# Where the tiles of a two-layer diffusion backbone begin in SBUF

## The chip, the cores and the metric

The kernel runs on one core of a Trainium2 chip. The metric is the device time of one execution in microseconds (us). A profile of one execution gives every instruction's start and length on each engine: PE (matmuls), PEld (the loads of a matmul's stationary operand, which overlap with PE), DVE, ACT, POOL, and SP, which issues most DMAs in the order in which they stand in its queue.

## The reference

A trunk of two layers (`DEPTH = 2`) works on 1024 latent tokens of width 1024, with 256 context tokens ahead of them in layer 0. All is float32. Cut to what matters here:

```python
# every layer: x = x + gate * norm(mixer(modulate(norm(x)))), then the same around a ConvFFN
# layer 0 (even): two mixers side by side
def attend(q, k, v):                                   # 8 query heads, 2 key heads, 64 wide, axial rotary
    s = jnp.einsum("bqhgd,bkhd->bhgqk", q, k).astype(jnp.float32) * ATTN_SCALE
    p = jax.nn.softmax(s, axis=-1).astype(v.dtype)
    return jnp.einsum("bhgqk,bkhd->bqhgd", p, v)
def step(S, inp):                                      # HGRN2, 4 heads, both directions, chunks
    ...
    o = jnp.einsum("bhts,bhsv->bhtv", scores, vc) + jnp.einsum("bhtd,bhdv->bhtv", qc * jnp.exp(b), S)
    S_new = jnp.exp(b_last[:, :, 0, :])[..., None] * S + jnp.einsum("bhsd,bhsv->bhdv", kc * jnp.exp(b_last - b), vc)
# layer 1 (odd): neighbourhood attention, 16 heads, 8 x 16 neighbours on a 64-wide grid, learned bias
# ConvFFN: up to 2 x 2816, a depthwise convolution of width 3 over the tokens, gate squared times value, down to 1024
```

## The kernel before, in words

Float32 operands are split into a high and a low part (names end in h and l, or _hi and _lo), and each product is three matmuls: high × high, high × low and low × high, accumulated in PSUM. In the rows of the profile a matmul reads `out<-moving,stationary`. Each matmul has its own load of 128 × 128 weights. Nearly all matmuls go through the helper on line 113, so all of them have the line L113, and one has to go by the names of their tiles.

The stages follow one another in this way. Times are those of the stretches of the profiled execution:

| stretch, us | stage | matmuls that carry it |
|---|---|---|
| 0–123 | modulation from `c_in`, first norm | `mod_ps<-m_raw,csil` |
| 123–254 | token-major projections of layer 0 (queries, keys, values, inputs), `mmB` | `g_ps<-w_hi,xh` and its two companions |
| 254–734 | bidirectional recurrence (`hgrn`) with its projections, `mmA` | `g_ps<-xh,w_hi` between many small ones |
| 734–1113 | even attention; its output projection runs between heads, its tail alone at the end | `a_pt`, `a_pv`, `g_ps<-w_hi,a_oh` |
| 1160–1730 | FFN-up of layer 0 | `u_g`, `u_v`, `u_pc` |
| 1730–2010 | FFN-down of layer 0 | `d_ps<-d_Bh,d_Ah` |
| 2030–2155 | values of layer 1, `mmB` | `g_ps<-w_hi,xh` |
| 2155–2543 | neighbourhood attention with its projections, `mmA` | `c_s`, `c_pt`, `c_pv`, `g_ps<-xh,w_hi` |
| 2606–2704 | output projection of layer 1 (`out_proj`) | `g_ps<-w_hi,a_oh` |
| 2750–3205 | FFN-up of layer 1 | `u_g`, `u_v` |
| 3205–3440 | FFN-down of layer 1 | `d_ps<-d_Bh,d_Ah` |

FFN-up is a Strassen-like scheme of seven products for each of 22 values of j: A11·B11, A12·B21, S2·T2, S1·T1, S3·T3, A22·T4 and S4·B22. A are halves of the weights and S sums of them; B are quarters of the normed input and T sums of them. One product is 4 slices of 128 rows, three matmuls of 512 columns each:

```python
                self.mm(ps, h, xhk, start and i == 0, False)
                self.mm(ps, h, xlk, False, False)
                self.mm(ps, lo, xhk, False, stop and i == len(jobs) - 1)
```

So 84 matmuls of 128x512 make one j. In layer 0 the context tokens add 48 of 128x256 (`u_pc`). While PE works on one j, ACT and POOL split and add the weights of the next, and DVE adds products, applies the convolution, and squares (`f_u`, `f_t`).

The order of the instructions on PE, ACT, DVE and POOL is the order in which the program writes them (`in_order`), and each engine works through its own row. SP's queue is first in, first out. A tile's place in SBUF is set by its pool: pools are stacked, some from the left edge of SBUF and some (`side="right"`: the weights, `nx`) from the right edge, and within a pool one tile follows the other. So a small tile shifts the start of everything that is stacked behind it. The pool `const` at the far left holds `mhalf` (the exponent −0.5 of line 121); behind it, on its side, stand `small`, the modulation's tiles and each stage's.

The tiles that the change touches: `mhalf` (L70); `c_in` (L164, the conditioning vectors, loaded first of all and passed through Silu into `csil`, the stationary operand of the modulation's matmuls); `onw` (L523, the norm's weight in `hgrn`, one value per partition, read on L822 by `h_o`); `zeros` (L1019, in even attention); `cw` (L1306, the convolution's weights in FFN-up).

Of the kernel before, what the change touches and what calls it, by code (L numbers as in the profile page):

```python
# [11 lines left out]
F32 = mybir.dt.float32  # L12
# [3 lines left out]
OP = mybir.AluOpType  # L16
# [4 lines left out]
P = 128  # L21
D = 1024
KT = D // P
# [13 lines left out]
EPS = 1e-6  # L37
HGRN_SCALE = 128 ** -0.5
NEG = -1.0e30


BLOCKS = ((0, 512), (512, 512), (1024, 256))
# [2 lines left out]
def vap(t, off, dims):  # L45

    b = t[:]
    return bass.AP(tensor=b.tensor, offset=b.offset + off, ap=[list(b.ap[0])] + [list(d) for d in dims])


class Homes:

    def __init__(self, first, second, names):
        self.first, self.second, self.names = first, second, names
# [6 lines left out]
class Trunk:  # L61
    def __init__(self, tc, a, out, es):
        self.tc, self.nc, self.a, self.out = tc, tc.nc, a, out
        nc = self.nc
        pool = lambda n, b, **k: es.enter_context(tc.tile_pool(name=n, bufs=b, **k))
        self.cp = pool("const", 1)
        self.dp = pool("scratch", 1, space=DRAM)
        self.ident = self.cp.tile([P, P], F32, name="ident")
        make_identity(nc, self.ident)
        self.mhalf = self.cp.tile([P, 16], F32, name="mhalf")  # L70
        nc.vector.memset(self.mhalf, -0.5)
        self.small = pool("small", 8)
        d = lambda n, s, t=F32: self.dp.tile(s, t, name=n)
        self.q2d = d("q2d", [AQ, P, NTOK], F32R)
        self.k2d = d("k2d", [AKV, 2, P, NTOK], F32R)
        self.v2d = d("v2d", [NT, P, AKV * P], F32R)
        self.bid = d("bid", [NT, P, 512])
        self.hgd = d("hgd", [BH, P, NTOK])
        self.gated = d("gated", [DEPTH, 2, 2, D])
        self.x1d = d("x1d", [NTOK, D])  # L80
        self.x2d = d("x2d", [NTOK, D])
        self.x3d = d("x3d", [SEQ, D])
        self.actd = d("actd", [FK, P, NTOK])
        self.vcd = d("vcd", [NT, P, CH * P], F32R)
        self.ocd = d("ocd", [KT, P, SEQ])
        self.ed = d("ed", [CH, 8, 31, 24])
        self.mod = {}
        self.fill_offset = 600
        E = mybir.EngineType
        self.compute = (E.PE, E.Activation, E.DVE, E.Pool)  # L90
# [70 lines left out]
    def mod_init(self):  # L161
        nc, a = self.nc, self.a
        self.csil = self.mc.tile([P, KT, 32], F32, name="csil")
        c = self.mc.tile([P, KT, 2], F32, name="c_in")  # L164
        nc.sync.dma_start(c, a["cc"])
        nc.vector.memset(self.csil, 0.0)
        nc.scalar.activation(self.csil[:, :, 0:2], c, AF.Silu)
        self.bmt = self.mc.tile([P, DEPTH, 48], F32, name="bmt")
        nc.sync.dma_start(self.bmt, a["bmodT"])
        self.nrm = self.mc.tile([P, DEPTH, 2, KT], F32, name="nrm")  # L170
        nc.sync.dma_start(self.nrm, a["npreT"])
# [341 lines left out]
    def hgrn(self, xh, xl, gp, tp, pp, sp, mods):  # L513
# [4 lines left out]
        nc, a = self.nc, self.a  # L518
# [1 line left out]
        M2 = sp.tile([P, 5, 32], F32, name="hM2", bufs=1)  # L520
        nc.sync.dma_start(M1, a["hM1"])
        nc.sync.dma_start(M2, a["hM2"])
        onw = sp.tile([P, 1], F32, name="onw", bufs=1)  # L523
        nc.sync.dma_start(onw, a["out_norm"])
        ones = sp.tile([P, P], F32, name="ones", bufs=1)
        nc.vector.memset(ones, 1.0)
        WD = 512
# [68 lines left out]
        def chain(u):  # L596

            st = U[u]
            n, nch, F, K, q = st["n"], st["nch"], st["F"], st["K"], st["q"]
# [11 lines left out]
            while m <= 64:  # L611
                if m <= 16:
                    KM = sp.tile([P, WD], F32, name="hKM", tag="hKM", bufs=2)
                    nc.scalar.copy(vap(KM, 0, ((2 * m, n // (2 * m)), (m, 2), (1, m))),
                                   vap(K, 0, ((2 * m, n // (2 * m)), (WD + m, 2), (1, m))))
                yield
                if m == 1:
                    for c in range(nch):
                        for i in range(4):
                            b = c * P + 32 * i  # L620
                            self.mm(pd[c // 2][32 * i:32 * i + 32, c % 2, 4, :], kd[:, b:b + 32], q[:, b:b + 32], True, True,
                                    tile_position=(0, 32 * i))
                if m <= 16:
                    slot = {8: 0, 4: 1, 2: 2, 1: 3}.get(m)
                    for c in range(nch):
                        for i in range(4):
                            b = c * P + 32 * i
                            o = pa[32 * i:32 * i + 32, c, 32 * i:32 * i + 32] if m == 16 else \
                                pd[c // 2][32 * i:32 * i + 32, c % 2, slot, :]
                            self.mm(o, KM[:, b:b + 32], vap(Q, b, ((2 * m, 16 // m), (WD + m, 2), (1, m))), True, True,  # L630
                                    tile_position=(0, 32 * i))
                else:
                    for c in range(nch):
                        for b in range(0, P, 2 * m):
                            l, r = slice(b, b + m), slice(b + m, b + 2 * m)
                            gl, gr = slice(c * P + b, c * P + b + m), slice(c * P + b + m, c * P + b + 2 * m)
                            self.mm(pa[l, c, r], K[:, 0, gl], Q[:, 1, gr], True, True, tile_position=(0, b))
                            self.mm(pa[r, c, l], K[:, 1, gr], Q[:, 0, gl], True, True, tile_position=(0, b + m))

                nb = n // (2 * m)  # L640
                tt, o = (F, 0) if m == 1 else (T, toff[m])

                ko = vap(K, 0, ((WD + m, 2), (2 * m, nb), (1, m)))
                nc.vector.tensor_tensor(out=ko, in0=ko, in1=vap(tt, o + 1, ((WD - 1, 2), (2, nb), (0, m))), op=OP.mult)
                qo = vap(Q, 0, ((WD + m, 2), (2 * m, nb), (1, m)))
                nc.vector.tensor_tensor(out=qo, in0=qo, in1=vap(tt, WD + o + 1, ((-WD - 1, 2), (2, nb), (0, m))), op=OP.mult)
                nc.vector.tensor_tensor(out=vap(T, toff[2 * m], ((WD, 2), (1, nb))), in0=vap(tt, o, ((WD, 2), (2, nb))),
                                        in1=vap(tt, o + 1, ((WD, 2), (2, nb))), op=OP.mult)
                m *= 2
            tot = st["tot"] = sp.tile([P, 2, 4], F32, name="htot", bufs=3)  # L650
            nc.vector.tensor_copy(tot[:, :, :nch], vap(T, 504, ((WD, 2), (1, nch))))
            while tails:
# [21 lines left out]
            for i in range(len(pd)):  # L674
                k = min(2, nch - 2 * i)
                nc.vector.tensor_tensor(out=T5[:, 2 * i:2 * i + k], in0=pd[i][:, :k],
                                        in1=M2.unsqueeze(1).to_broadcast([P, k, 5, 32]), op=OP.mult)
# [101 lines left out]
    def hgrn_out(self, st, dirs, part, tp, pp, sp, onw, ones):  # L779
        nc = self.nc  # L780
        n0, n, nch = st["n0"], st["n"], st["nch"]
# [14 lines left out]
        if part == "keep":  # L796
            o = st["part"] = sp.tile([P, 512], F32, name="h_part", bufs=1)
# [3 lines left out]
        if part is None:  # L801
            o = sp.tile([P, 512], F32, name="h_o", bufs=1)
            nc.scalar.copy(o[:, :n], pof[:, :n])
        else:
            o = part
# [13 lines left out]
        pb = tp.tile([P, 512], F32, name="h_bc", tag="tp")  # L819
        self.mm(pb[:, :n], ones, dg.rearrange("p c n -> p (c n)")[:, :n], True, True)  # L820
        yield
        nc.vector.scalar_tensor_tensor(out=o[:, :n], in0=pb[:, :n], scalar=onw, in1=o[:, :n], op0=OP.mult, op1=OP.mult)  # L822
        nc.gpsimd.tensor_tensor(out=o[:, :n], in0=o[:, :n], in1=st["gate"][:, :n], op=OP.mult)
        yield
        nc.gpsimd.dma_start(self.hgd[st["h"]][:, n0:n0 + n], o[:, :n])
# [2 lines left out]
    def even_attention(self, gp, tp, pp, sp):  # L828
# [5 lines left out]
        nc, a = self.nc, self.a  # L834
# [181 lines left out]
                    next(fill, None)  # L1016
                    at[0] += 1

        zeros = sp.tile([P, 1], F32, name="zeros", bufs=1)  # L1019
        nc.gpsimd.memset(zeros, 0.0)  # L1020
        N = 2 * len(pairs)
        E = mybir.EngineType
# [175 lines left out]
    def ffn_up(self, l, src, ctx, x_src, x_dst, hp, pp, tp, es, beside):  # L1198


        nc, a = self.nc, self.a
# [84 lines left out]
        with self.in_order(*self.compute), ExitStack() as loads:  # L1286
# [16 lines left out]
            for f in early:  # L1303
                f()
            sp = self.pool(es, f"fu{l}", 2)
            cw = sp.tile([P, 44, 4], F32, name="cw", bufs=1)  # L1306
            nc.sync.dma_start(cw, a["convT"][l])
            load(1, 0)
            first(0)
# [7 lines left out]
            for j in range(FK):  # L1317
                n = j + 1
# [801 lines left out]
    def pool(self, es, n, b=1, **k):  # L2120
        k.setdefault("reuse_waits", "tile")
        return es.enter_context(self.tc.tile_pool(name=n, bufs=b, **k))
# [117 lines left out]
def shape_constants():  # L2240
# [21 lines left out]
    full = np.broadcast_to(rowok[:, :, None], (P, 16, 24))  # L2262
    c["rmask"] = order(np.where(full, 0.0, -NEG).astype(np.float32))
    full = np.broadcast_to(colok[:, None, :], (P, 16, 24))
    c["cmask"] = order(np.where(full, 0.0, -NEG).astype(np.float32))
    return c
# [52 lines left out]
```

## Time and profile before

| | |
|---|---|
| median of 3 runs | 3436.86 us (3434.71 to 3441.72) |
| profiled execution, span | 3440.7 us, 48748 instructions (its own time is not given beside it) |
| mean granted TensorE clock | 0.957 |
| PE busy | 91% of the span |
| weight loads busy | 75% |
| DVE, POOL, ACT busy | 60%, 44%, 43% |
| mean DMA rate | 116 GB/s |

The page gives for each engine the time in which it was busy. Matmuls overlap in the pipeline: one of 512 columns is recorded with some 0.39 us, while the next one starts after some 0.23. So what a stream of matmuls costs is read from the distance between starts, and not from the recorded length. The chain of work that ended last merges a stream of matmuls into one piece with its length and count, and length divided by count is that distance.

### The profile page before, as it was taken

To read this page: it belongs to the slowest core of one execution; us is meant where nothing else is said; L and a number is where in the kernel's file an instruction comes from. 1 tells how busy PE (TensorE), PEld (TensorE's weight loads), DVE (VectorE), ACT (ScalarE), POOL (GpSimd) and SP (SyncE) were. 2 spreads that over 40 slices of the span, in tenths; PEclk is the share of its full clock that TensorE was granted. 3 is DMA by queue.
4 is the path that set the end of the run, shared out by engine and by line. 5 is a ranking of instruction groups with operands and counts; after the bars stand their busy time and mean duration, and the time that the engine had idled before them with its cause. 6 is when DMAs were issued, how large, how long until landed. Compare 5 with 4: busy or idle time off the path is not lost.

```text
span 3440.7 us, 48748 instructions
## 1 busy us (share of the span) xinstructions
PE 3141.5 (91%) x18364; PEld 2565.3 (75%) x18364; DVE 2058.2 (60%) x3413; ACT 1486.8 (43%) x2619; POOL 1525.8 (44%) x1147
## 2 busy tenths in 40 slices
PE   5899998869998699999999989999997679999997
PEld 2767676658887488888878768898986468888785
DVE  3624666657775754544577862476775565554778
ACT  3322222256664543434344442566664343333443
POOL 1310111187774466666610111677771167777201
PEclk7999999979999799999999999999998799999998
DMA  6524333221112211212285772222216412222756
GB/s 232 154 97 136 118 127 117 101 89 38 50 44 71 96 68 62 70 68 72 74 290 193 259 233 108 70 61 64 64 45 185 138 61 80 74 86 80 266 184 217
DMA packets 203948, 399.25 MB, mean 116 GB/s; under 512 B 23216, under 2 KB 85168, under 8 KB 203712
## 3 DMA queue, kind: packets, MB, share of 16 engines
q1 hardware_dynamic: 194656, 364.15, 32.4%
q0 software_dynamic: 9056, 31.99, 2.4%
q8 instruction: 144, 2.36, 0.3%
q14 instruction: 92, 0.75, 0.1%
HBM read 322.11 MB, written 74.34 MB: 115 GB/s over the span
## 4 chain that ended last, share of the span: by engine, by line
PE 75%; DVE 10%; DMA 4%; ACT 4%; issue 4%; POOL 2%; SPq 0%; POOLq 0%; ACTq 0%; DVEq 0%
PE g_ps L113 21%; PE u_g L113 13%; PE d_ps L113 11%; PE u_v L113 10%; PE u_pc L113 3%; PE a_pv L113 2%; PE c_pv L113 2%; PE c_s L113 2%; PE c_pt L2028 2%; PE a_pt L926 2%; PE mod_ps L113 1%; DVE a_pl L928 1%; PE a_s L113 1%; ACT a_ph L927 1%; DMA y_x<-x2d 1%
## 5 line engine op out<-in xcount | busy, mean ns | idle before, releaser
L121 POOL TENSOR_TENSOR rs_r<-rs_e,mhalf 128x1 f32<-128x1 f32 (+3 forms) x106 | 81.4, 768 | 1018.4 <-DVE rs_e L120 1018.2
L113 PE MATMUL d_ps<-d_Bh,d_Ah 128*128 128x512 f32 x704 | 276.9, 393 | 11.4 <-ACT d_Bh L1456 10.9
L113 PE MATMUL g_ps<-xh,w_hi 128*128 128x512 f32 (+1 forms) x704 | 278.8, 396 | 4.4 <-ACT w_hi L543 4.4
L113 PE MATMUL d_ps<-d_Bl,d_Ah 128*128 128x512 f32 x704 | 277.6, 394 | 2.9 <-DVE d_Bl L1457 2.4
L113 PE MATMUL d_ps<-d_Bh,d_Al 128*128 128x512 f32 x704 | 276.4, 393 | 1.7 <-DVE d_Al L1457 1.6
L906 POOL TENSOR_SCALAR a_p<-a_p,rl 128x1280 f32<-128x1280 f32 (+1 forms) x80 | 240.3, 3008 | 69.9 <-DVE rl L905 61.7
L2011 POOL TENSOR_SCALAR c_p<-c_p,rl 128x640 f32<-128x640 f32 (+1 forms) x128 | 231.1, 1807 | 85.8 <-DVE rl L2010 62.5
L113 PE MATMUL g_ps<-xh,w_lo 128*128 128x512 f32 (+1 forms) x704 | 259.4, 368 | 1.4 <-DVE w_lo L544 1.4
L113 PE MATMUL g_ps<-xl,w_hi 128*128 128x512 f32 (+1 forms) x704 | 259.3, 368 | 0.0
L1238 DVE TENSOR_TENSOR f_u<-u_v,f_p 128x512 f32<-128x512 f32 x88 | 60.5, 688 | 199.0 <-PE u_v L113 199.0
L928 DVE TENSOR_TENSOR a_pl<-a_pt,a_ph 128x512 fp32r<-128x512 f32 (+1 forms) x200 | 118.6, 602 | 88.7 <-ACT a_ph L927 88.3
L113 PEld LDWEIGHTS g_ps<-xh,w_hi 128*128 128x128 f32 x704 | 135.7, 193 | 44.0 <-issue 27.7
L113 PEld LDWEIGHTS d_ps<-d_Bh,d_Ah 128*128 128x128 f32 x704 | 133.4, 189 | 41.6 <-ACT d_Bh L1456 12.1
L1224 POOL TENSOR_TENSOR w_S4l<-w_s,w_S4h 128x512 fp32r<-128x512 f32 x44 | 57.2, 1301 | 240.2 <-ACT w_S4h L1223 236.3
L113 PEld LDWEIGHTS d_ps<-d_Bl,d_Ah 128*128 128x128 f32 x704 | 133.6, 190 | 34.5 <-DVE d_Bl L1457 6.7
L113 PE MATMUL g_ps<-w_hi,xh 128*128 128x512 f32 (+1 forms) x400 | 156.0, 390 | 2.2 <-DVE xh L1793 1.2
L113 PEld LDWEIGHTS d_ps<-d_Bh,d_Al 128*128 128x128 f32 x704 | 133.5, 190 | 30.6 <-DVE d_Al L1457 3.1
L113 PE MATMUL g_ps<-w_lo,xh 128*128 128x512 f32 (+1 forms) x400 | 151.8, 379 | 3.9 <-DVE w_lo L1781 3.2
L927 ACT CAST a_ph<-a_pt 128x512 fp32r<-128x512 f32 (+1 forms) x200 | 102.8, 519 | 119.4 <-PE a_pt L926 119.4
L113 PEld LDWEIGHTS g_ps<-xh,w_lo 128*128 128x128 f32 x704 | 135.2, 192 | 25.6 <-DVE w_lo L544 1.9
L113 PE MATMUL g_ps<-w_hi,xl 128*128 128x512 f32 (+1 forms) x400 | 151.8, 380 | 0.2 <-DVE xl L278 0.2
L2031 DVE TENSOR_TENSOR c_pl<-c_pt,c_ph 128x256 fp32r<-128x256 f32 (+1 forms) x256 | 113.0, 470 | 50.4 <-ACT c_ph L2030 49.0
(468 smaller groups left out, 9734.2 us busy)
## 6 DMA issues: line engine op xcount, KB each, us to landing
m_raw<-in_w_mod SPq DMA_DIRECT2D x96, 512.0 KB
w_raw<-in_w_up SPq DMA_DIRECT2D x88, 512.0 KB
d_rawA<-actd SPq DMA_DIRECT2D x77, 512.0 KB
d_rawB<-in_w_down SPq DMA_DIRECT2D x74, 512.0 KB
actd<-f_t SPq DMA_DIRECT2D x22, 640.0 KB
d_t<-in_w_down SPq DMA_DIRECT2D x22, 512.0 KB
actd<-f_t SPq DMA_DIRECT2D x22, 512.0 KB
d_s<-actd SPq DMA_DIRECT2D x20, 512.0 KB
```

The lines of the kernel that those rows point to most:

```text
L113: return self.nc.tensor.matmul(out, lhsT, rhs, start=start, stop=stop, skip_group_check=True, **k)
L121: nc.gpsimd.tensor_tensor(out=r[:p, :n], in0=e[:p, :n], in1=self.mhalf[:p, :n], op=OP.pow)
L906: nc.gpsimd.tensor_scalar(Pt[:, :nk], Pt[:, :nk], rl, None, op0=OP.mult)
L926: nc.tensor.transpose(pt[:, m, qt * P:(qt + 1) * P], Pt[:, kts[j + m] * P:(kts[j + m] + 1) * P], self.ident)
L927: nc.scalar.copy(ph[:, j:j + n], pt[:, :n])
L928: nc.vector.tensor_tensor(out=pl[:, j:j + n], in0=pt[:, :n], in1=ph[:, j:j + n].bitcast(F32), op=OP.subtract)
L1224: nc.gpsimd.tensor_tensor(out=lo, in0=part(j, name), in1=hi.bitcast(F32), op=OP.subtract)
L1238: nc.vector.tensor_tensor(out=out, in0=x, in1=y, op=OP.add)
L2011: nc.gpsimd.tensor_scalar(Pt[:, :n], Pt[:, :n], rl, None, op0=OP.mult)
L2028: nc.tensor.transpose(pt[:, j, :], Pt[:, (src + j) * P:(src + j + 1) * P], self.ident)
L2031: nc.vector.tensor_tensor(out=vap(pl, o, dims), in0=pt[:, :cnt], in1=vap(ph, o, dims).bitcast(F32), op=OP.subtract)
```

## The change

Five small tiles are padded or moved, so that what stands behind them begins at a multiple of 128 bytes. `LINE = 32` float32 values are 128 bytes.

- `mhalf` leaves the left edge for a pool of its own at the right edge, 24 values wide and not 16.
- `c_in` gets 4 values in place of 2 for each of its 8 groups, of which the first 2 are used.
- `onw` is allocated, and its DMA issued, at the end of `hgrn`'s first chain and no longer ahead of its first weight loads.
- `zeros` is 32 values wide, of which one is used.
- `cw` has 48 groups of 4 in place of 44.

```diff
+LINE = 32
...
-        self.mhalf = self.cp.tile([P, 16], F32, name="mhalf")
+        self.ep = es.enter_context(tc.tile_pool(name="edge", bufs=1, side="right"))
+        self.mhalf = self.ep.tile([P, 24], F32, name="mhalf")
...
-        c = self.mc.tile([P, KT, 2], F32, name="c_in")
+        c = self.mc.tile([P, KT, 4], F32, name="c_in")[:, :, 0:2]
         nc.sync.dma_start(c, a["cc"])
...
-        onw = sp.tile([P, 1], F32, name="onw", bufs=1)
-        nc.sync.dma_start(onw, a["out_norm"])
+        onw = []
...
+            if not onw:
+                onw.append(sp.tile([P, 1], F32, name="onw", bufs=1))
+                nc.sync.dma_start(onw[0], a["out_norm"])
             tot = st["tot"] = sp.tile([P, 2, 4], F32, name="htot", bufs=3)
...
-        nc.vector.scalar_tensor_tensor(out=o[:, :n], in0=pb[:, :n], scalar=onw, in1=o[:, :n], op0=OP.mult, op1=OP.mult)
+        nc.vector.scalar_tensor_tensor(out=o[:, :n], in0=pb[:, :n], scalar=onw[0], in1=o[:, :n], op0=OP.mult, op1=OP.mult)
...
-        zeros = sp.tile([P, 1], F32, name="zeros", bufs=1)
+        zeros = sp.tile([P, LINE], F32, name="zeros", bufs=1)[:, 0:1]
...
-            cw = sp.tile([P, 44, 4], F32, name="cw", bufs=1)
+            cw = sp.tile([P, 48, 4], F32, name="cw", bufs=1)[:, 0:44, :]
```

In the built programs the tiles begin at these bytes of a partition; one place of several is shown where a tile is given more than one, and all of them agree modulo 128 but where it is said.

| tiles | before | modulo 128 | after | modulo 128 |
|---|---|---|---|---|
| weights w_raw, w_hi, w_lo, all stages | 167904 | 96 | 167808 | 0 |
| FFN-up weights A, e.g. w_A11h | 180192 | 96 | 180096 | 0 |
| FFN-up sums S, e.g. w_S1h | 124032 | 0 | 124032 | 0 |
| FFN-up B11, B21, e.g. x_B110h | 25024 | 64 | 24960 | 0 |
| FFN-up T2, T3, T4, e.g. x_T20h | 74176 | 64 | 74112 | 0 |
| FFN-up T1, B22, e.g. x_T10h | 212960 | 96 | 212864 | 0 |
| FFN-up context, x_ctx0h | 20928 | 64 | 20864 | 0 |
| FFN-down d_Ah | 25024 | 64 | 24960 | 0 |
| FFN-down d_Bh | 53696 | 64 | 53632 | 0 |
| even attention a_oh, V2, a_ph | 102880 (a_oh) | 96 | 102912 | 0 |
| layer 1 a_oh | 25024 | 64 | 24960 | 0 |
| xh and xl of layer 0 | 22528 | 0 | 22528 | 0 |
| xh and xl of layer 1 | 20928 | 64 | 20864 | 0 |
| hgrn hq | 120480 | 32 | 120448 | 0 |
| mhalf | 17024 | 0 | 229248 | 0 |
| onw | 105600 | 0 | 157312 | 0 |

On PE, ACT, DVE and POOL the instructions stand in the same order before and after. On SP one row moves. Around the start of `hgrn` (hM are its masks, w_raw its first four weights, hV its values), SP's queue before is:

```order
L521 DMA hM_1994<-in_hM 128x128
L522 DMA hM_1995<-in_hM 128x160
L524 DMA onw<-in_out_norm 128x1
L536 DMA w_raw_2004<-in_w_fm 128x1024
L536 DMA w_raw_2006<-in_w_fm 128x1024
L536 DMA w_raw_2008<-in_w_fm 128x1024
L536 DMA w_raw<-in_w_fm 128x1024
L594 DMA hV<-bid 128x2x128
L594 DMA hV<-bid 128x4x128
```

And after, at the same place of SP's queue:

```order
L523 DMA hM_1997<-in_hM 128x128
L524 DMA hM_1998<-in_hM 128x160
L537 DMA w_raw_2005<-in_w_fm 128x1024
L537 DMA w_raw_2007<-in_w_fm 128x1024
L537 DMA w_raw_2009<-in_w_fm 128x1024
L537 DMA w_raw<-in_w_fm 128x1024
L595 DMA hV<-bid 128x2x128
L653 DMA onw<-in_out_norm 128x1
L595 DMA hV<-bid 128x4x128
```

The load of `onw` went from ahead of the four weight loads to behind the first load of hV.

The first rows of SP's queue, with the modulation's loads, before:

```order
L165 DMA c_in<-in_cc 128x16
L169 DMA bmt<-in_bmodT 128x96
```

And after:

```order
L167 DMA c_in<-in_cc 128x8x2
L171 DMA bmt<-in_bmodT 128x96
```

The order is the same, but the first load now writes 8 separate pairs in each partition and not one row of 16.

## The prediction

> **What bounds the kernel now.** I began with the first part of the page, the busy time of each engine, and with its fourth part, the chain of work that ended last.
>
> ```profile
> PE 3141.5 (91%) x18364; PEld 2565.3 (75%) x18364; DVE 2058.2 (60%) x3413; ACT 1486.8 (43%) x2619; POOL 1525.8 (44%) x1147
> PE 75%; DVE 10%; DMA 4%; ACT 4%; issue 4%; POOL 2%; SPq 0%; POOLq 0%; ACTq 0%; DVEq 0%
> PE g_ps L113 21%; PE u_g L113 13%; PE d_ps L113 11%; PE u_v L113 10%; PE u_pc L113 3%; PE a_pv L113 2%; PE c_pv L113 2%; PE c_s L113 2%; PE c_pt L2028 2%; PE a_pt L926 2%; PE mod_ps L113 1%; DVE a_pl L928 1%; PE a_s L113 1%; ACT a_ph L927 1%; DMA y_x<-x2d 1%
> ```
>
> PE carries 75% of the chain, and four groups (g_ps, u_g, d_ps, u_v) carry 55% of the span. So what moves the time is how often PE can start a matmul. Next the table of stretches: us, then PE, weight load, DVE, ACT and POOL, then granted clock, DMA share, GB/s.
>
> ```profile
> 277.00:665.00 388.00, 363.55 (x4043) 269.09 (x4041) 241.34 (x518) 109.00 (x205) 50.46 (x66) 0.99 0.36 116
> 1160.00:1730.00 570.00, 557.59 (x2904) 472.88 (x2903) 293.39 (x333) 226.44 (x327) 361.11 (x262) 0.99 0.20 70
> 2750.00:3205.00 455.00, 435.59 (x1857) 350.39 (x1856) 244.94 (x247) 181.77 (x264) 328.51 (x240) 0.98 0.24 81
> ```
>
> Both FFN-up stretches (1160 and 2750) are PE's from their first microseconds on, POOL the next busiest at 63% and 72%, at nearly full granted clock. Where matmuls follow one another without a stop, the chain in order of time (start, us, matmuls) gives their rate, since a piece's length divided by its count is the distance between two starts:
>
> ```profile
> 3205.74 185.29 PE d_ps L113 x816
> 2810.62 8.38 PE u_g L113 x36
> 2819.00 2.75 PE u_v L113 x12
> 2821.75 2.80 PE u_g L113 x12
> 2824.55 5.56 PE u_v L113 x24
> 1303.36 2.84 PE u_pc L113 x24
> 1306.20 2.80 PE u_g L113 x12
> 1309.00 2.76 PE u_v L113 x12
> 1311.76 2.83 PE u_pc L113 x24
> 1314.59 2.80 PE u_g L113 x12
> 1317.39 5.56 PE u_v L113 x24
> 1322.95 5.59 PE u_g L113 x24
> 207.77 11.20 PE g_ps L113 x48
> ```
>
> All but u_pc are 128x512 matmuls of one type, yet they have three rates. d_ps goes every 227.1 ns (185.29/816). u_g of the first row goes every 232.8, at 2821.75 and in token-major g_ps (11.20/48) every 233.3. The S2·T2 product (2.75/12) lies between, at 229.2. I laid the start addresses of the two operands beside them (table in the section on the change), modulo 128, moving operand first: d_ps is 64 and 64; token-major 96 and 0; S1·T1 96 and 0; A12·B21 64 and 96; S2·T2 64 and 0. At 227 the two starts are equal, at 233 they are 32 off modulo 64, and at 229 they are 64 apart. One stream tests this away from the FFN: the tail of even attention's output projection, where both begin at 96. On the timeline these are the ends of 67 consecutive matmul rows:
>
> ```profile
> 1090.81 0.39 PE L113 MATMUL g_ps<-w_hi,a_oh 128*128 128x512 f32 x1
> 1105.77 0.39 PE L113 MATMUL g_ps<-w_hi,a_oh 128*128 128x512 f32 x1
> ```
>
> That is 14.96/66 = 226.7 ns, with no operand at a multiple of 128. So misalignment by itself costs PE nothing here; a difference between the two operands does, by up to 6.2 ns of 233.3. The change makes every large operand begin at 0, hence all differences 0. That is the case for a gain.
>
> **The change, part by part.**
>
> *FFN-up of layer 1.* One pass over j is 84 matmuls in 8.38 + 2.75 + 2.80 + 5.56 = 19.49 us. At d_ps's rate it is 84 × 0.2271 = 19.07. 22 passes: −9.1 us, all on the path, since PE has no gap between these pieces. What is late next is DVE: its last step of a pass frees the u_v that T3·S3 writes.
>
> ```profile
> 2823.14 0.68 DVE L1238 TENSOR_TENSOR f_u<-u_v,f_p 128x512 f32<-128x512 f32 x1
> 2824.39 0.39 PE L113 MATMUL u_v<-x_T30h,w_S3h 128*128 128x512 f32 x1
> ```
>
> It ends at 2823.82, 0.57 before PE needs it. The 60 matmuls of the pass in between shrink by some 0.3, so about 0.27 is left: it still fits.
>
> *FFN-up of layer 0.* The 512-wide parts of a pass are 2.80 + 2.76 + 2.80 + 5.56 + 5.59 = 19.51, against 19.07: 22 × 0.44 = −9.7. The 48 u_pc matmuls (256 wide, 5.67 us, 118.1 ns each) have 64 against 96, and yet not slower than the equal-phase 256-wide a_pv of even attention:
>
> ```profile
> 803.20 0.28 PE L113 MATMUL a_pv<-a_ph,V 128*128 128x256 f32 x1
> 804.28 0.28 PE L113 MATMUL a_pv<-a_pl,V 128*128 128x256 f32 x1
> ```
>
> Ten rows, 1.08/9 = 120 ns. So u_pc gains nothing, and at worst loses 48 × 1.9 ns × 22 = 2.0. I take +0.5, near zero because a_pv's stream is a broken one: −9.2 for the stage.
>
> *Token-major and out_proj.* The counts are those of the grouped rows (whole program, by form); x512 belongs to the two interrupted stages below:
>
> ```profile
> L113 PE MATMUL g_ps<-w_hi,xh 128*128 128x512 f32 x320 | 130.2, 407 | 2.2 <-DVE xh L1793 1.2 <-ACT w_hi L477 1.0
> L113 PE MATMUL g_ps<-w_hi,a_oh 128*128 128x512 f32 x288 | 124.6, 436 | 12.6 <-ACT w_hi L131 12.5
> L113 PE MATMUL g_ps<-xh,w_hi 128*128 128x512 f32 x512 | 217.6, 425 | 0.0
> ```
>
> Three such kinds each: 960 matmuls of token-major and layer 1's values at 233.3 − 227.1 = 6.2 ns are 6.0 us. Some 1/5 goes back to waits on w_lo and xh that end by DVE's clock and not PE's: −4.8. Out_proj has 384 (the other 480 of the x288 kinds are even attention's, equal already): 2.4, of which I take half, because its chain is partly transfers:
>
> ```profile
> 2646.22 5.03 DMA y_x<-x2d
> ```
>
> So −1.2, bounds 0 and −2.4.
>
> *Recurrence and neighbourhood attention.* 1536 matmuls, 32 off, but cut into short runs between other work:
>
> ```profile
> 300.03 2.10 PE g_ps L113 x9
> 800.14 0.70 PE g_ps L113 x3
> ```
>
> Both are 233.3 ns, the first 32 off, the second (even attention) equal. By these two nothing is gained; by the steady rate 1536 × 6.2 = 9.5. I take −2.5, nearer the short runs, since that is what these streams are; bounds 0 and −9.5.
>
> *FFN-down, transposes, scores.* FFN-down goes from 64/64 to 0/0, no difference before or after: 0. Nothing covers it; if 0/0 isn't like 64/64 this is where it shows (rival 3).
>
> *ACT, DVE, POOL.* Their operations move to aligned starts too. By form, ACT's cast from and to 96 and its cast from and to 0:
>
> ```profile
> L1223 ACT CAST w_A11h<-w_raw 128x512 fp32r<-128x512 f32 x44 | 27.2, 619 | 0.0
> L1223 ACT CAST w_S2h<-w_s 128x512 fp32r<-128x512 f32 x44 | 27.3, 621 | 129.9 <-POOL w_s L1217 129.9
> ```
>
> 619 against 621 ns: the start alone is worth 0 there.
>
> *onw.* Its DMA leaves the place ahead of the four weight loads, for which PE stands waiting:
>
> ```profile
> 257.46 0.43 SPq L524 DMA_DIRECT2D onw<-in_out_norm  x1
> 257.93 1.87 SPq L536 DMA_DIRECT2D w_raw<-in_w_fm  x4
> 264.24 0.43 PE L113 MATMUL g_ps<-xh,w_hi 128*128 128x256 f32 x1 [2.71 <-ACT w_hi L543]
> ```
>
> The loads are issued 0.47 earlier (257.93 − 257.46): −0.5. Behind the first hV load it holds only later hV and m_raw loads up by 0.43; nothing waits for onw before the first h_o, so 0 there.
>
> *c_in.* It grows a gap in each row, so its DMA writes 1024 pieces of 8 bytes and not 128 of 64. The first silu waits for it, PE for the silu:
>
> ```profile
> q1 hardware_dynamic: 194656, 364.15, 32.4%
> 3.81 0.22 ACT L167 ACTIVATE csil<-c_in 128x16 f32<-128x16 f32 x1
> 6.58 5.51 PE L113 MATMUL mod_ps<-m_raw,csil 128*32 128x512 f32 x16 [6.58 <-DMA m_raw<-in_w_mod]
> ```
>
> A packet takes 0.324 × 16 × 3440.7/194656 = 0.092 us in the mean, so 896 more over 16 engines are at most 5.1 us; silu would end at 9.1 and not 4.03, 2.6 after PE's start at 6.58, and the weight loads queued behind it could be as late. Tiny packets should cost less than the mean, and 2.5 us of slack are there: +0.5, bounds 0 and +5.1.
>
> *mhalf, zeros, cw.* Larger or moved, same instructions: 0.
>
> **The sum.** −9.1 − 9.2 − 4.8 − 1.2 − 2.5 − 0.5 + 0.5 = −26.8. The profiled execution's span of 3440.7 becomes 3413.9. The three runs shown have their median 3.8 lower, at 3436.86, and this gives 3410.1 there. The three runs lie within 7.0 us of each other, 0.2%, which I take as what a measurement can tell from no change.
>
> [...]
>
> **The rivals.**
>
> 1. *The rate isn't set by the starts.* What d_ps and the attention tail share may be something else: who reads beside them, PSUM, the kind of program around. Then nothing gains: 3436.86 + 0.5 − 0.5 = 3437. For it: all phases sit in different stages, so start and stage are mixed. Against it: S2·T2 and S1·T1 stand side by side in a pass, beside the same engines, with 2.75 and 2.80 us in both layers, and differ in the starts. Chance 0.10.
>
> 2. *Two operands at 0 act like S2·T2 (one at 0, one at 64), 229.2 ns.* FFN-up gains 3696 × (232.1 − 229.2) = 10.7, token-major, values, out_proj and the attention streams about 5, FFN-down (3 × 704 matmuls) loses 2112 × 2.1 = 4.4: −11, or 3426. Chance 0.08.
>
> 3. *The other side: a start at 0 itself costs.* No row of before at 227 ns has an operand at 0: those pairs are 64/64 and 96/96. If 0/0 goes at 233.3, FFN-down loses 2112 × 6.2 = 13.1, FFN-up 3696 × 1.2 = 4.4, others nothing: +17, or 3454. It decides from a 0/0 rate above 231.3 ns, the mean over those 2112 at 227.1 and the 6576 others (mean 232.6). Against it: A12·B21 needs 233 with no operand at 0. Chance 0.06.
>
> 4. *DVE's slack of 0.57 is used up* in some passes (PE then stands before T3·S3): of 18 us in FFN-up some 5 return: 3415. Chance 0.15.
>
> 5. *The interrupted streams gain all their 9.5*: 7 more, 3403. Chance 0.15.
>
> **How the numbers follow.** The forecast, 3410, has 0.46. With 4, 5 and rival 2, faster is 0.84; the same is rival 1, 0.10; slower is rival 3, 0.06. The range leaves out rivals 1 and 3 (0.16): from 3399 (rival 5, with c_in and u_pc at 0 and out_proj in full) to 3427 (rival 2, rounded up).
>
> **What would show it.** In the chain after: u_g x36 near 8.18, u_v x12 and u_g x12 both near 2.73, u_v x24 near 5.45, the token-major x48 near 10.90, d_ps x816 still near 185.3. If u_g x12 stays at 2.80, rival 1; if d_ps goes to 187, rival 2; to 190, rival 3. A wait of T30 on f_u in most passes shows rival 4. The first mod_ps after 6.58, with csil as what it waited for, shows c_in's price. The w_raw issue near 257.5, relative to what precedes it, shows onw's.
>
> The forecast is wrong if the first rows show equal-start matmuls at any rate but 226 to 228 ns.

## The result, and the profile after

The kernel became faster by 0.6%: 3419.2 us median (3412.62 to 3424.98, 4 runs) against 3439.27 (3434.71 to 3441.72, 4 runs), ratio 0.9941 with a 95% interval of 0.9925 to 0.9957. That is 20 us, where 27 were forecast; 3410 was the predicted time and 3399 to 3427 the range. Run again beside three experiments the changed kernel took 3415.48 (ratio 0.994, 0.9926 to 0.9954).

The busy times and the chain of the page hardly show it:

```profile
PE 3125.8 (91%) x18364; PEld 2575.7 (75%) x18364; DVE 2057.6 (60%) x3413; ACT 1486.6 (43%) x2619; POOL 1524.0 (45%) x1147
PE 74%; DVE 10%; DMA 4%; ACT 4%; issue 4%; POOL 2%; SPq 1%; POOLq 0%; ACTq 0%; DVEq 0%
```

PE is busy 16 us less with the same 18364 matmuls. The chain in order of time (start, us, matmuls) says where. One pass of FFN-up in layer 1, one in layer 0, then FFN-down, token-major of layer 0 and the values of layer 1:

```profile
2808.58 2.72 PE u_v L115 x12
2811.30 2.72 PE u_g L115 x12
2814.02 5.49 PE u_v L115 x24
2819.51 8.16 PE u_g L115 x36
1298.99 2.87 PE u_pc L115 x24
1301.86 2.75 PE u_g L115 x12
1304.61 2.72 PE u_v L115 x12
1307.33 2.87 PE u_pc L115 x24
1310.20 2.75 PE u_g L115 x12
1312.95 5.44 PE u_v L115 x24
1318.39 5.44 PE u_g L115 x24
1744.52 163.29 PE d_ps L115 x719
203.81 11.19 PE g_ps L115 x48
2108.02 36.76 PE g_ps L115 x162
```

Most 512-wide matmuls of FFN-up now go at 226.7 ns (8.16/36), as d_ps did and does (163.29/719 = 227.1). The exceptions are small: u_g behind u_pc (2.75/12 = 229.2) and the piece that begins with T3·S3 (5.49/24 = 228.8). The values of layer 1 go at the new rate as well (36.76/162 = 226.9). One of their pieces before, and the same piece after (15.40/66 = 233.3 and 15.00/66 = 227.3 ns):

```profile
2086.03 15.40 PE g_ps L113 x66
2076.73 15.00 PE g_ps L115 x66
```

Two rows don't fit: token-major of layer 0 still takes 233.1 ns (11.19/48) though both its operands begin at a multiple of 128, and u_pc went from 118.1 to 119.6 ns (2.87/24).

This table gives the time between the first matmuls of the stages, and for the two parts of even attention and for neighbourhood attention to their last ones, from the timelines of two profiles of each kernel (the second profiles are from the runs told of below). The row of the values ends at the first scores of neighbourhood attention, so it holds 30 us of that stage's projections:

| stage | before, us | after, us | mean change |
|---|---|---|---|
| start to token-major | 50.66, 47.55 | 47.26, 49.90 | −0.5 |
| token-major, layer 0 | 205.20, 202.41 | 204.56, 201.36 | −0.8 |
| recurrence | 478.11, 475.94 | 473.09, 473.83 | −3.6 |
| even attention to its last a_pv | 353.29, 354.80 | 356.81, 354.44 | +1.6 |
| tail of its output projection | 25.76, 25.76 | 26.38, 26.38 | +0.6 |
| FFN-up, layer 0 | 570.54, 570.47 | 564.24, 563.35 | −6.7 |
| values, layer 1 | 155.14, 155.13 | 152.67, 152.42 | −2.6 |
| neighbourhood attention | 409.06, 408.99 | 409.96, 407.99 | 0 |
| out_proj and norm, layer 1 | 145.81, 145.84 | 146.66, 142.55 | −1.2 |
| FFN-up, layer 1 | 453.43, 452.99 | 445.15, 445.76 | −7.8 |

The rest, both FFN-downs, norms and the ends, adds 1.2. The spans are 3440.7 and 3434.4 before, 3423.0 and 3412.5 after, 19.8 apart in the mean. Both FFN-ups and the values repeat within 1 us, and the tail to the digit, so these are the change's. The early stages, even attention and out_proj differ by up to 4 us between two profiles of one kernel, so what their rows show isn't told apart from that.

### The profile page after: what moved, and what is told of

It reads as the page before. It is cut to its first block, busy times and chain, and to the rows that moved or that the text cites. A ratio compares the mean times of both kernels' runs of the same rounds, so it can differ in the third digit from the quotient of the medians.

```text
span 3423.0 us, 48746 instructions
## 1 busy us (share of the span) xinstructions
PE 3125.8 (91%) x18364; PEld 2575.7 (75%) x18364; DVE 2057.6 (60%) x3413; ACT 1486.6 (43%) x2619; POOL 1524.0 (45%) x1147
## 2 busy tenths in 40 slices
DMA packets 204844, 399.25 MB, mean 117 GB/s; under 512 B 24112, under 2 KB 86064, under 8 KB 204608
## 4 chain that ended last, share of the span: by engine, by line
PE 74%; DVE 10%; DMA 4%; ACT 4%; issue 4%; POOL 2%; SPq 1%; POOLq 0%; ACTq 0%; DVEq 0%
PE g_ps L115 21%; PE u_g L115 13%; PE d_ps L115 10%; PE u_v L115 10%; PE u_pc L115 4%; PE c_pv L115 2%; PE a_pv L115 2%; PE c_s L115 2%; PE c_pt L2032 2%; PE a_pt L930 2%; PE mod_ps L115 1%; DVE a_pl L932 1%; PE a_s L115 1%; ACT a_ph L931 1%; DMA m_raw<-in_w_mod 1%
```

## The experiments

Two theories for the rows that don't fit. D: the rate is set by the distance of the two operands' starts (that of the moving one less that of the stationary one, called its weights below) modulo 256 and not modulo 128. After the change xh of layer 0 begins at 22528, which is 0 modulo 256, but w_hi at 167808, which is 128; in FFN-up, FFN-down and the values all operands are 128 modulo 256. L: multiples of 128 are what counts, and something else holds token-major.

### The changed kernel once more

> The changed kernel once more, for a second profile and a time that shares its runs of before with the next three. Both theories: ratio 0.994, inside 0.9925 to 0.9957. In its chain u_g x36 at 8.16 us, token-major x24 at 5.60. What is asked is how far the stages that the change should not touch repeat: even attention, whose span from the first a_s to the last a_pv was 353.3 us before and 356.8 after.

Measured: 3415.48 us, ratio 0.994; the stages are in the table above. Even attention took 354.4 this time: its first profile's 3.5 us too many don't repeat.

### Distance 0 in layer 0's mixer too

```diff
-    def weights(self, es, raw, split):
+    def weights(self, es, raw, split, pad=0):
         self.w_raw, self.w_hi = raw, split
+        if pad:
+            es.enter_context(self.tc.tile_pool(name="w_pad", bufs=1, side="right")).tile([P, pad], F32, name="w_pad")
...
-                self.weights(e2, 2, 5)
+                self.weights(e2, 2, 5, LINE)
...
-                self.weights(e2, 1, 4)
+                self.weights(e2, 1, 4, LINE)
...
-            self.weights(es, 2, 8)
+            self.weights(es, 2, 8, LINE)
```

> The changed kernel with the right-hand weights of layer 0's mixer (token-major, recurrence, even attention) moved down by 128 bytes; all starts stay multiples of 128. Theory D (the distance of the two operands' starts modulo 256 sets the rate): these stages have 128 between weights and xh or a_oh now and 0 here, so token-major g_ps x24 goes from 5.60 us to 5.45, the output projection's tail back to 227 ns, and the recurrence's 512-wide matmuls in dense stretches from 232.4 towards 227; 3 to 7 us faster than the changed kernel. Theory L (multiples of 128 are what counts, and something else holds these stages): x24 stays 5.60, no gain.

Measured: 3414.14 us (3407.12 to 3421.38), ratio 0.9929 (0.9915 to 0.9944). The chain in token-major:

```profile
194.79 5.46 PE g_ps L115 x24
200.69 10.93 PE g_ps L115 x48
212.62 16.55 PE g_ps L115 x72
```

10.93/48 = 227.7 ns where the changed kernel has 233.1. The tail of even attention's projection is back at 25.76 us. Token-major as a whole took 199.4 us. In the recurrence the undisturbed 512-wide steps fell from 232.4 to 230.0 ns in the mean, and its stage took 472.9 us, as without: there PE waits for others (in the changed kernel it is busy for 414.3 of the 474.0 us from 254 to 728). So D for the rates. The time missed its expectation: 1 us less by the medians and not 3 to 7, which the intervals can't separate from 0.

### Distances kept, all starts off the multiples of 128

```diff
-        self.mhalf = self.ep.tile([P, 24], F32, name="mhalf")
+        self.edge = self.ep.tile([P, 8], F32, name="edge")
+        self.mhalf = self.cp.tile([P, 16], F32, name="mhalf")
```

> The changed kernel with mhalf back at the left (64 bytes) and 32 bytes at the right edge in place of its 96: all large operands begin 64 past a multiple of 128, and all distances between operands are those of the changed kernel. Theory D: the time of the changed kernel within 4 us, u_g x36 at 8.16. Theory L: back to before, u_g x36 at 8.38, ratio 1.00.

Measured: 3416.55 us, ratio 0.9936 (0.9924 to 0.9947). One pass of FFN-up in layer 1:

```profile
2803.28 2.72 PE u_v L116 x12
2806.00 2.72 PE u_g L116 x12
2808.72 5.46 PE u_v L116 x24
2814.18 8.16 PE u_g L116 x36
```

The whole gain, with no large operand at a multiple of 128. L falls.

### All at multiples of 128, but 128 apart

```diff
-        self.mhalf = self.ep.tile([P, 24], F32, name="mhalf")
+        self.mhalf = self.ep.tile([P, 56], F32, name="mhalf")
```

> The changed kernel with mhalf 56 values wide and not 24: everything stacked at the right begins 128 bytes lower, all starts stay multiples of 128. In FFN-up five of the seven products (all but S2·T2 and S3·T3) now have 128 between their operands. Theory D: these go to about 232.3 ns as token-major has after, u_v x12 of S2·T2 stays at 2.72; FFN-up loses 60 x 22 x 2 x 5.5 ns = 14.5 us, layer 1's values and out_proj some 4, and layer 0's mixer gains 3 to 7: 10 to 15 us slower than the changed kernel. Theory L: no change from it.

Measured: 3431.72 us (3428.23 to 3438.57), ratio 0.9982 (0.9973 to 0.999): 16 us slower than the changed kernel beside it, where 10 to 15 were expected. Its pass:

```profile
2808.02 2.76 PE u_v L115 x12
2810.78 2.79 PE u_g L115 x12
2813.57 5.53 PE u_v L115 x24
2819.10 8.39 PE u_g L115 x36
```

233.1 ns (8.39/36) with every start a multiple of 128. FFN-up took 572.0 and 453.5 us, as before the change. Another miss: S2·T2, whose operands I left equal, takes 2.76 and not 2.72. Its twelve steps, the mean by place in the product over the passes from 2800 to 3150 us, show why (start to start, from the timelines, ns):

```
changed kernel, S2·T2, distance 0, neighbours too      227 227 227 227 227 227 227 227 227 227 227 227
off128, S2·T2, distance 0 between others at 128        233 236 224 231 236 228 232 231 227 227 227 227
off128, S4·B22, distance 128                           234 229 238 229 238 229 238 229 238 229 238 229
off128, A11·B11, distance 128                          230 232 241 233 231 232 228 230 232 241 232 236
before, A11·B11, distance 224                          235 232 235 232 235 232 235 232 235 232 235 233
before, S2·T2, distance 64                             229 232 226 229 232 226 229 232 226 229 232 226
```

Here the equal pair needs eight matmuls to settle at 227 after its neighbours; T3·S3, the other equal pair of this run, needs three. A distance repeats a pattern, but not always the same one: both rows at 128 have a mean of 233 ns.

### Distance 64

```diff
-        self.mhalf = self.ep.tile([P, 24], F32, name="mhalf")
+        self.mhalf = self.ep.tile([P, 40], F32, name="mhalf")
```

> The changed kernel with mhalf 40 values wide: everything at the right begins 64 bytes lower, so five of FFN-up's seven products have 64 between their operands. Theory D as S2·T2 of before had it (steps of 226, 229 and 232 in turn): those products at 2.75 us per 12, u_g x36 at 8.25; FFN-up loses 60 x 22 x 2 x 2.4 ns = 6 us, about a third of what 128 cost. Rival, that any distance but 0 costs the same: u_g x36 at 8.38.

Measured, one run: 3425.71 us, FFN-up 566.5 and 452.4, together 10 us more than in the changed kernel's two profiles, where 6 were expected. Its pass:

```profile
2803.08 2.74 PE u_v L115 x12
2805.82 2.80 PE u_g L115 x12
2808.62 5.49 PE u_v L115 x24
2814.11 8.34 PE u_g L115 x36
```

Neither: the sign counts. Where the moving operand begins 64 after the weights, in A11·B11 and A22·T4, the steps go 229, 232, 226 again; where it begins 64 before them (S1·T1 and S4·B22, distance 192) every step of this layer is 233. The expectation left out that this edit makes both signs. One product shows that the distance isn't all: A12·B21 has 64 too, but comes straight behind S4·B22 here and keeps its 233 ns (232.7 in the mean over the passes), while in layer 0, where it follows u_pc, it falls into 229, 232, 226 after three steps. So a pair can carry on the steps of the pair before it.

### One operand of three

```diff
-            xl = hp.tile([P, KT, NTOK], F32R, name="xl")
+            xl = hp.tile([P, KT * NTOK + 2 * LINE], F32R, name="xl")[:, LINE:LINE + KT * NTOK].rearrange("p (k n) -> p k n", k=KT)
```

The edit is the one in `odd_in`, layer 1.

> The changed kernel with layer 1's xl begun 128 bytes further on (its tile is larger by 256, so nothing else changes modulo 256). In layer 1's values the three matmuls of a slice are w_hi on xh, w_lo on xh, w_hi on xl, with xh, xh, xl as weights. If what counts is the moving operand against the weights loaded beside it, those of the next matmul, the second of each three is the slow one; if it is against the matmul's own weights, the third. In either case their mean lies between 227 and 233 ns, g_ps x24 between 5.45 and 5.60.

Measured, one run: 3423.69 us; the piece of 162 matmuls takes 37.46 us, 231.2 ns each. Consecutive starts on its timeline:

```profile
2110.23 0.39 PE L115 MATMUL g_ps<-w_hi,xh 128*128 128x512 f32 x1
2110.46 0.40 PE L115 MATMUL g_ps<-w_lo,xh 128*128 128x512 f32 x1
2110.69 0.40 PE L115 MATMUL g_ps<-w_hi,xl 128*128 128x512 f32 x1
2110.93 0.39 PE L115 MATMUL g_ps<-w_hi,xh 128*128 128x512 f32 x1
```

The means over the stage are 228 ns after w_hi on xh, 232 after w_lo on xh (xl is loaded beside it: in the changed kernel's profile that load and the matmul of w_lo on xh both start at 2110.16, the matmul with xl at 2110.39) and 234 after w_hi on xl. Both take longer, so this doesn't tell a matmul's own weights from the next one's. One weight tile in three at another distance costs two steps in three.

### Before, a second profile

> The kernel before once more, for a second profile. Asked is which differences between the stages of before and after are the change's. If the recurrence's 4 to 5 us (478.1 before, 473 to 474.6 in five profiles of changed kernels) are the change's, this profile has 478 again; if they are pauses for instructions or of the clock that fall now here and now there, it has something else, 473 to 476. FFN-up repeats within 0.5 us in both cases (570.5 and 453.4).

Measured: 3436.22 us. The recurrence took 475.9 us, 2.2 less than in the first profile; FFN-up 570.5 and 453.0. Most of the spread in the recurrence is one pause. In the first profile of before PE stood for 2.4 us with the engine itself as the cause:

```profile
675.85 0.44 PE L113 MATMUL h_pa<-hQ,hK 128*32 128x32 f32 x15 [2.43 <-issue]
```

In the changed kernel's the same place has 0.34. Without this pause the first profile of before would have 476 as well. The eight profiles with the change, experiments included, have 472.9 to 475.8 (the next run 475.5). So a gain of the recurrence from the change isn't shown.

### Everything together

```diff
-        c = self.mc.tile([P, KT, 4], F32, name="c_in")[:, :, 0:2]
+        c = self.mc.tile([P, 2, KT, 2], F32, name="c_in")[:, 0]
...
-                X[name, k // 2] = [hp.tile([P, 2 * n], F32R, name=f"x_{name}{k // 2}{x}", bufs=1) for x in "hl"]
+                at = lambda x: 8 if (name, k, x) == ("ctx", 0, "h") else 0
+                end = lambda x: 56 if (name, k, x) == ("ctx", 6, "l") else 0
+                X[name, k // 2] = [hp.tile([P, at(x) + 2 * n + end(x)], F32R, name=f"x_{name}{k // 2}{x}",
+                                           bufs=1)[:, at(x):at(x) + 2 * n] for x in "hl"]
```

In this form the first context tile begins 32 bytes further on too, by its slice, so every context operand is 32 past its weights. The weights' pad of match256 is kept.

> match256 with two things more: c_in's load is one row of 64 bytes again (its tile keeps its size, so no start moves), and layer 0's context tiles x_ctx, but for the first, begin 32 bytes past the others. Theory D with what the traces have shown since: u_pc x24 goes from 2.87 us back to 2.83 (128x256 matmuls went slightly faster with starts 32 apart), 1.5 us in all; the first mod_ps starts 0.3 earlier, at 6.6. With match256's 427 ns of the token-major triples kept, 3410 to 3415 us, ratio 0.992 to 0.993. Rival: a 128x256 matmul doesn't depend on the distance and u_pc stays 2.87.

Measured: 3411.63 us (3407.95 to 3415.88), ratio 0.9925 (0.9913 to 0.9937), the lowest median of all; its interval still overlaps that of the changed kernel. FFN-up of layer 0 took 560.3 us, 3 to 4 less than in the changed kernel:

```profile
1299.85 2.80 PE u_pc L115 x24
1302.65 2.75 PE u_g L115 x12
1305.39 5.44 PE u_v L115 x24
```

u_pc goes at 116.7 ns 32 apart and at 119.6 with equal starts. So equal starts, the best for the 512-wide matmuls, aren't the best for these 256-wide ones. It is not simply the opposite: off128, where u_pc has 128 between its operands, shows 120.2 (2.88 and 2.89 for 24).

```profile
1293.48 2.88 PE u_pc L115 x24
1301.92 2.89 PE u_pc L115 x24
```

## Why the prediction was right, and where it wasn't

**FFN-up, layer 1**: −9.1 forecast, −7.8 measured. The mechanism and the rate are as said: a pass went from 19.49 to 19.09 us (2.72 + 2.72 + 5.49 + 8.16). What fails is "22 passes, all on the path": in the first passes PE still waits for others, and the stretch from the stage's start to T3·S3 of the second pass took 52.65 us before and 52.62 after. Some 20 dense passes are left, 20 × 0.40 = −8.0. DVE's slack, forecast to shrink from 0.57 to 0.27, did:

```profile
2812.95 0.68 DVE L1242 TENSOR_TENSOR f_u<-u_v,f_p 128x512 f32<-128x512 f32 x1
2813.68 0.19 PEld L115 LDWEIGHTS u_v<-x_T30h,w_S3h 128*128 128x128 f32 x1
2813.86 0.40 PE L115 MATMUL u_v<-x_T30h,w_S3h 128*128 128x512 f32 x1
```

f_u ends at 2813.63, 0.23 before the matmul. It fits, but barely: the weight load starts only 0.05 behind f_u's end, 0.18 before its matmul where its neighbours have 0.23, in nearly every pass. T3·S3's steps begin at 233, 230, 231 ns in the mean over the passes, and u_v x24 takes 5.44 to 5.49 in them, where 24 × 226.7 is 5.44. Rival 4's place was right, its price not: some 0.03 a pass, and not 5 us in 44 passes, which is 0.11.

**FFN-up, layer 0**: −9.2 against −6.7. The 512-wide parts fell to 19.10 (2.75 + 2.72 + 2.75 + 5.44 + 5.44), 0.41 less a pass. Two terms were mis-sized. One is u_pc: +0.07 a pass, +1.5 us and not +0.5. The other is the number of passes, as in layer 1: a dense pass went from 25.18 to 24.84 us, and 20 of them give −6.8. a_pv's 120 ns, which I set aside as that of a broken stream, was the right row.

**Token-major and values**: −4.8 against −2.6 for the values and nothing that can be told for layer 0. The part of the values was 2.4 of the forecast and came true; that of token-major, 2.4 too, is the step that failed. Its sign, the x48 near 10.90, came out at 11.19. The prediction's last line calls it wrong if equal starts go at any rate but 226 to 228 ns; modulo 128, as it counted them, that happened here. "The change makes every large operand begin at 0, hence all differences 0" holds modulo 128, and the rows were sorted modulo 128. The addresses in the table would have given 0 against 128 modulo 256 for token-major, the recurrence and the attention's tail. But no pair of before had that distance, so its price couldn't have been read there; off128 (233.1 against 226.7 ns) and match256 (233.1 against 227.7) put it at 5 to 6 ns in dense stretches. The tail, left out as equal already, lost 0.6 us: its distance went from 0 to 128.

**out_proj**: −1.2 forecast and, in the mean of two, measured. That is luck: the two profiles of the changed kernel differ by 4 us.

**Recurrence and neighbourhood attention**: −2.5 forecast. Neighbourhood attention gave 0; its distance is 0 now, but its runs are mostly of three matmuls, and their steps went only from 232.8 to 231.5 ns. The recurrence's −3.6 isn't the rate's, since its distance only went from 32 to 128 and match256's 0 didn't shorten it; its runs of nine are about as long as the settling in off128. So that the total lies within 7 us of the forecast is luck in part: 3.6 of the 20 come from pauses and unsettled differences of the recurrence, where the forecast had a rate.

**onw**: −0.5, as forecast. The weight loads follow the last mask load directly, 0.47 after its start, and PE's first matmul on these weights starts 6.9 after that load, where it was 7.3 and 7.7 in the two profiles of before:

```profile
252.95 0.42 SPq L524 DMA_DIRECT2D hM<-in_hM  x1
253.42 1.95 SPq L537 DMA_DIRECT2D w_raw<-in_w_fm  x4
```

**c_in**: +0.5 forecast, some +0.3 measured, by another way. The silu does end later, 4.92 and not 4.03, but nothing waits for it. What counts is the issue: c_in's takes 0.70 us for 0.39 and the next one, bmt's, 0.64 for 0.42, and m_raw's loads stand behind them on SP, 2.62 for 2.10:

```profile
0.72 0.70 SPq L167 DMA_DIRECT2D c_in<-in_cc  x1
1.47 0.64 SPq L171 DMA_DIRECT2D bmt<-in_bmodT  x1
2.62 1.85 SPq L180 DMA_DIRECT2D m_raw<-in_w_mod  x4
4.70 0.22 ACT L169 ACTIVATE csil<-c_in 128x16 f32<-128x16 f32 x1
6.79 1.07 PE L115 MATMUL mod_ps<-m_raw,csil 128*32 128x512 f32 x2 [6.79 <-DMA m_raw<-in_w_mod]
```

The whole program has 896 packets more (204844 for 203948), priced at up to 5.1 us. ACT, which waits for c_in, starts at 3.40 and not 2.51, 0.89 later, so tiny packets did cost less than the mean of 0.092 us each. PE starts with m_raw at 6.79, where it was 6.58; the second profiles have 6.87 and 6.39. With one row of 64 bytes (best) the issue is 0.39 again and the start 6.52.

**Rivals.** FFN-down kept its 227 ns at 0/0, so rivals 2 and 3 fall; FFN-up's 226.7 removes rival 1, and off128 and shift64 confirm it. Rival 5 falls with the interrupted streams, which gained next to nothing (232.8 to 231.5 ns a step in neighbourhood attention).

One sum of the prediction is off: the lower end of its range, rival 5 with c_in and u_pc at 0 and out_proj in full, adds up to 3401 and not 3399. Nothing hangs on it.

## What to carry to other kernels

In a dense stream of matmuls (runs of three gained next to nothing here, 232.8 to 231.5 ns), compare start-to-start distances of the same shape in different stages; where they differ by 2 to 3% with no wait in the trace (here 233.1 against 226.7 ns), write down the two operands' addresses. Align operands to each other, modulo 256 bytes here (128 apart went at 233.1 ns in off128), and not to a round address (shift64 has 3416.55 us, the changed kernel 3415.48); a padding that aligns one stage can misalign another (the attention's tail went from 25.76 to 26.38 us), so list every pair. A pattern found modulo one number should be sorted by its multiples too before it is priced.

## What the runs showed of the hardware

All figures here are measured in the profiles and runs of this case. The distance in bytes from the start of the stationary operand to that of the moving one, modulo 256, and the mean step of 128x512 matmuls in dense stretches:

- 0: 226.7 to 227.1 ns once settled (FFN-up after, 8.16/36 = 226.7; FFN-down after, 163.29/719 = 227.1).
- 64: 229 to 230 ns (S2·T2 before, 2.75/12 = 229.2), but for A12·B21 of layer 1 in off64 (232.7).
- 32, 96, 128, 192 and 224: 232 to 233.6 ns (32: values before, 15.40/66 = 233.3; 96: S1·T1 before, 2.80/12 = 233.3; 128: off128, 8.39/36 = 233.1; 192: S1·T1 in off64, 2.80/12 = 233.3; 224: token-major before, 11.20/48 = 233.3).

160 wasn't tried. The start itself makes no difference here: all at 0 (again, 3415.48 us) and all at 64 modulo 128 (shift64, 3416.55) take the same. A pair with distance 0 settles only after some matmuls, three to eight in off128. 128x256 matmuls have another order in u_pc: 119.7 ns at 0 (after), 120.1 at 128 (off128), 116.8 at 32 (best), 117.8 at 64 (off64), 118.1 at 224 (before). Why the distance counts stays open: xl128 lengthened the step of the matmul beside the load (232 ns) and of the one that uses it (234), against 228 for the third.
